# A decoder trunk on Trainium2: the low parts of its weights by an accumulating transfer in place of a subtraction on GpSimd

## The chip, the cores and the metric

The kernel runs on one core of a Trainium2 chip. The metric is the time of one execution in device microseconds (us). Lower is better. The engines are named as the profile names them: PE is TensorE (PEld its weight loads), DVE is VectorE, ACT is ScalarE, POOL is GpSimd, SP is SyncE (SPq its queue of transfers).

## What is computed

Four layers of a decoder over 1024 tokens of width 1024, in float32. The mixer of layer i is of kind i mod 3: gated linear attention (layers 0 and 3), a spatial gating unit (layer 1), forgetting attention (layer 2).

```
for i in range(DEPTH):                                   # DEPTH = 4
    mod = (silu(c) @ w_mod[i] + b_mod[i])[:, None, :]
    shift, scale, gate = split(mod, 3)
    h = rms_norm(x, norm_pre_g[i]) * (1.0 + scale) + shift
    kind, j = i % N_MIXERS, i // N_MIXERS
    ...                                                  # o = mixer(h @ w_in), times silu(z), @ w_out
    x = x + gate * rms_norm(o, norm_post_g[i])
```

The products `h @ w_in` and `o @ w_out` carry most of the work: w_in has 3088, 3072 or 4112 columns, w_out 1024.

## The kernel before

**Three matmuls for one.** The projections run in float32r, in which one matmul takes less time than in float32 but rounds its operands. Both operands are split into a rounded high part and a low part, the remainder: activations into hTh and hTl, weights into whi and wlo. `mm3` (L283) sums three products: high by high (L285), and the two of high by low (L286, L287). `proj_tok` (L289) and `proj_feat` (L324) call it for eight slices of the inner dimension (kt 0 to 7) and leave the sum in a PSUM bank (pool pj, three banks).

**Weights.** Each layer's weights are cut into blocks of about 256 columns, planned in order by `plan` (L273) and `plan_out` (L394). `getw` (L276) keeps one block ahead of the one in use. `load_w` (L246) fetches a block in two halves p4, each of 512 rows: a transfer by SyncE into a raw tile `wraw` (L263, 128 partitions x 4 x 256 floats, 512 KB), and then `split` (L251): ScalarE rounds the raw tile into the high part (L254), GpSimd subtracts it from the raw tile and writes the low part (L255). There are 176 halves in the program. The pool of `wraw` has two buffers, so a raw load waits until the subtraction two halves earlier has read its tile. The pool of `whi` and `wlo` (tag whl) has eight buffers, two for each half: a block in use and the next one. A cast therefore waits until the matmuls have done with the same half of the block two back. In the opening, wide transfers of the modulation weights (L182) use buffers of this pool too.

**Stages.** A layer runs through its input blocks, with the mixer's work put between the projections, and then through `out_proj` (L399): two halves of the tokens, four blocks each, so eight blocks a layer; in each block four tiles of 128 tokens, 24 matmuls for a tile. After each tile VectorE multiplies the bank by the gate (L410) and ScalarE squares it (L412), both to free the bank. Beside it `post` (L422) adds the residual of the tokens finished before and prepares the next layer's activations.

**Other work named below.** L197 accumulates the modulation on VectorE. L580 is a running sum, L602 to L612 the scaled operands of the gated attention's scores, L623 their matmuls, L625 copies them from PSUM under a mask. L673 to L683 update and read the attention's state (L678 on VectorE). L387 and L474 are low parts of activations on VectorE. L536 copies a few columns of a projection. L983 copies the halves of a tile between partitions by transfers within SBUF (L1019 and L1020 wait for them).

**What sets the order.** The kernel is written for a scheduler that simulates the program on a timeline and lays down the order of each engine's instructions; places marked high priority (L409) are preferred, and each engine then works strictly in its order and waits on semaphores. Transfers are all issued by SyncE, in the order of its queue.

Of the kernel before, what the change touches and what calls it, by code (L numbers as in the profile page):

```python
# [8 lines left out]
F32 = mybir.dt.float32  # L9
F32R = mybir.dt.float32r  # L10
U8 = mybir.dt.uint8
AF = mybir.ActivationFunctionType
ALU = mybir.AluOpType
# [15 lines left out]
class Trunk:  # L29
# [216 lines left out]
    def load_w(self, srcs, now=True):  # L246
        nc = self.nc
        ncol = sum(s.shape[1] for s in srcs)
        raws, parts = [], []

        def split(raw):  # L251
            hi = self.wp.tile([P, 4, ncol], F32R, tag="whl", name=self.nm("whi"))
            lo = self.wp.tile([P, 4, ncol], F32R, tag="whl", name=self.nm("wlo"))
            nc.scalar.copy(hi, raw)  # L254
            nc.gpsimd.tensor_tensor(lo, raw, hi.bitcast(F32), op=ALU.subtract)  # L255
            parts.append((hi, lo))

        for p4 in range(2):
            raw = self.wp.tile([P, 4, ncol], F32, tag="wraw", name=self.nm("wraw"), bufs=2)
            c = 0  # L260
            for s in srcs:
                w = s.shape[1]
                nc.sync.dma_start(out=raw[:, :, c:c + w],  # L263
                                  in_=s[p4 * 512:(p4 + 1) * 512, :].rearrange("(k p) n -> p k n", p=P))
                c += w
            if now:
                split(raw)
            else:
                raws.append(lambda raw=raw: split(raw))
        self.wdone.append(lambda kt: (parts[kt // 4][0][:, kt % 4, :], parts[kt // 4][1][:, kt % 4, :]))  # L270
        return raws
# [960 lines left out]
```

## Time and profile before

| | us |
|---|---|
| median of three runs | 2159.36 |
| lowest and highest | 2156.47 and 2163.68 |
| the profiled execution | 2157.83 |
| its span, first to last instruction | 2156.1 |
| PE busy in the span | 2093.7 (97%) |
| DVE busy | 1323.0 (61%) |
| ACT busy | 942.5 (44%) |
| POOL busy | 884.0 (41%) |
| mean busy share of the DMA engines, by SyncE's queue | 33.1% |

Busy time says how much of the span an engine held instructions. Matmuls overlap each other, so that PE counts as busy while it is only filled. What an engine that is not PE costs is read from the waits of PE, and those in turn from the timeline around them. The granted clock over the span is 0.992 of the full one.

### The profile page before, as it was taken

To read this page: it belongs to the slowest core of one execution; us is meant where nothing else is said; L and a number is where in the kernel's file an instruction comes from. 1 tells how busy PE (TensorE), PEld (TensorE's weight loads), DVE (VectorE), ACT (ScalarE), POOL (GpSimd) and SP (SyncE) were. 2 spreads that over 40 slices of the span, in tenths; PEclk is the share of its full clock that TensorE was granted. 3 is DMA by queue.
4 is the path that set the end of the run, shared out by engine and by line. 5 is a ranking of instruction groups with operands and counts; after the bars stand their busy time and mean duration, and the time that the engine had idled before them with its cause. 6 is when DMAs were issued, how large, how long until landed. Compare 5 with 4: busy or idle time off the path is not lost.

```text
span 2156.1 us, 39182 instructions
## 1 busy us (share of the span) xinstructions
PE 2093.7 (97%) x15173; PEld 1934.2 (90%) x15173; DVE 1323.0 (61%) x2940; ACT 942.5 (44%) x2041; POOL 884.0 (41%) x751
## 2 busy tenths in 40 slices
PE   6999999999999999999999999999899999999998
PEld 6888999999998889998888888888689999899998
DVE  7686878535475425555656656656766674776633
ACT  4655334345422114554445445445555655343342
POOL 5443333366344333645343244243326441332363
PEclk9999999999999999999999999999999999999999
DMA  8132323335425432524223224223425320111334
GB/s 291 40 93 74 94 85 98 122 115 180 146 77 160 143 105 98 175 83 109 74 74 109 79 69 115 72 70 108 134 88 196 100 59 21 50 59 55 118 106 144
DMA packets 183268, 225.91 MB, mean 105 GB/s; under 512 B 14290, under 2 KB 129554, under 8 KB 183082
## 3 DMA queue, kind: packets, MB, share of 16 engines
q1 hardware_dynamic: 183082, 223.41, 33.1%
q8 instruction: 119, 1.95, 0.4%
q14 instruction: 67, 0.55, 0.1%
HBM read 185.03 MB, written 29.95 MB: 100 GB/s over the span
## 4 chain that ended last, share of the span: by engine, by line
PE 83%; DVE 10%; ACT 2%; issue 2%; DMA 2%; POOL 0%; DVEq 0%; SPq 0%; POOLq 0%; ACTq 0%
PE pj L285 21%; PE pj L287 21%; PE pj L286 21%; PE pm L1056 4%; PE pm L1045 3%; PE pb L623 2%; DVE md L197 2%; PE pb L1019 2%; PE pb L1020 1%; DVE s L580 1%; DMA s<-s 1%; PE pm L364 1%; PE pm L683 1%; PE pm L682 1%; DVE s L612 1%
## 5 line engine op out<-in xcount | busy, mean ns | idle before, releaser
L285 PE MATMUL pj<-whi,hTh 128*128 128x256 f32 (+1 forms) x3072 | 891.8, 290 | 2.9 <-ACT junk L412 1.9
L287 PE MATMUL pj<-whi,hTl 128*128 128x256 f32 (+1 forms) x3072 | 880.7, 287 | 4.4 <-DVE hTl L474 2.1
L286 PE MATMUL pj<-wlo,hTh 128*128 128x256 f32 (+1 forms) x3072 | 881.2, 287 | 0.0
L255 POOL TENSOR_TENSOR wlo<-wraw,whi 128x1024 fp32r<-128x1024 f32 (+2 forms) x176 | 423.3, 2415 | 434.6 <-ACT whi L254 397.9
L285 PEld LDWEIGHTS pj<-whi,hTh 128*128 128x128 f32 x3072 | 590.3, 192 | 10.7 <-issue 3.3
L287 PEld LDWEIGHTS pj<-whi,hTl 128*128 128x128 f32 x3072 | 589.2, 192 | 10.0 <-DVE hTl L474 3.1
L286 PEld LDWEIGHTS pj<-wlo,hTh 128*128 128x128 f32 x3072 | 590.4, 192 | 5.3 <-issue 2.4
L285 PE MATMUL pj<-hTh,whi 128*128 128x512 f32 x640 | 255.3, 399 | 0.0
L287 PE MATMUL pj<-hTh,wlo 128*128 128x512 f32 x640 | 254.1, 397 | 0.0
L286 PE MATMUL pj<-hTl,whi 128*128 128x512 f32 x640 | 253.1, 395 | 0.0
L254 ACT CAST whi<-wraw 128x1024 fp32r<-128x1024 f32 (+2 forms) x176 | 178.0, 1012 | 110.2 <-PE pj L286 92.8
L197 DVE SCALAR_TENSOR_TENSOR md<-md,cond,md 128x512 f32<-128x512 f32 x184 | 171.2, 932 | 36.0 <-DMA md<-in_w_mod 34.1
L1013 POOL TENSOR_TENSOR db<-s,mneg 128x128 f32<-128x128 f32 x128 | 69.1, 548 | 271.0 <-DVE mx L1028 158.2
L1047 ACT COPY s<-pm 128x512 f32<-128x512 f32 (+2 forms) x192 | 87.6, 480 | 127.2 <-PE pm L1045 125.0
L287 PEld LDWEIGHTS pj<-hTh,wlo 128*128 128x128 f32 x640 | 120.8, 189 | 24.7 <-issue 0.9
L286 PEld LDWEIGHTS pj<-hTl,whi 128*128 128x128 f32 x640 | 121.0, 189 | 23.9 <-issue 0.7
L285 PEld LDWEIGHTS pj<-hTh,whi 128*128 128x128 f32 x640 | 120.9, 189 | 23.7 <-issue 0.7
L410 DVE TENSOR_TENSOR s<-pj,gg 128x256 f32<-128x256 f32 x128 | 53.5, 420 | 132.1 <-PE pj L287 132.0
L1034 ACT ACTIVATE p<-p,ng 128x256 f32<-128x256 f32 (+7 forms) x128 | 99.5, 777 | 79.5 <-DVE ng L1032 78.6
L1023 DVE CUSTOM_DVE_ANT_0 p<-pb,s 128x512 f32<-128x512 f32 (+3 forms) x160 | 82.4, 526 | 61.3 <-PE pb L1020 58.6
L1132 ACT ACTIVATE s<-pj 128x256 f32<-128x256 f32 (+1 forms) x96 | 43.8, 457 | 165.7 <-PE pj L287 157.6
L340 POOL TENSOR_TENSOR r<-r,neghalf 128x1 f32<-128x1 f32 (+2 forms) x104 | 113.0, 1092 | 6.7
(202 smaller groups left out, 3237.3 us busy)
## 6 DMA issues: line engine op xcount, KB each, us to landing
md<-in_w_mod SPq DMA_DIRECT2D x160, 256.0 KB
wraw<-in_gla_w_in SPq DMA_DIRECT2D x32, 512.0 KB
wraw<-in_gla_w_out SPq DMA_DIRECT2D x32, 512.0 KB
yd<-s SPq DMA_DIRECT2D x50, 256.0 KB
xd<-x SPq DMA_DIRECT2D x24, 512.0 KB
wraw<-in_sgu_w_in SPq DMA_DIRECT2D x24, 512.0 KB
x<-xd SPq DMA_DIRECT2D x24, 512.0 KB
wraw<-in_fox_w_in SPq DMA_DIRECT2D x48, 256.0 KB
```

Of the source, the lines that this page charges most:

```text
L197: ins = nc.vector.scalar_tensor_tensor(st["acc"], w[i], self.cond[:, kt:kt + 1], st["acc"], op0=ALU.mult, op1=ALU.add)
L254: nc.scalar.copy(hi, raw)
L255: nc.gpsimd.tensor_tensor(lo, raw, hi.bitcast(F32), op=ALU.subtract)
L285: nc.tensor.matmul(ps, lh, rh, start=first, stop=False)
L286: nc.tensor.matmul(ps, lh, rl, start=False, stop=False)
L287: nc.tensor.matmul(ps, ll, rh, start=False, stop=last)
L340: nc.gpsimd.tensor_tensor(r, r, self.half[:, 0:1].to_broadcast([P, n]) if n > 8 else self.half[:, 0:n], op=ALU.pow)
L1013: nc.gpsimd.tensor_tensor(db, nf[p, ib // 4, hb][:, qc], mneg, op=ALU.add)
L1023: nc.vector.tensor_tensor_reduce(e[:, c * 512:c * 512 + d0], sp[:, 0:d0], nf[p, c, hb][:, 0:d0], op0=ALU.add, op1=ALU.max, scale=1.0, scal ...
L1034: nc.scalar.activation(e[:, 0:n + P], e[:, 0:n + P], AF.Exp, bias=ng, accum_out=ls[:, 0:1])
L1047: nc.scalar.copy(et[:, 0:nb * P], pt[:, 0:nb * P])
L1056: nc.tensor.matmul(po[own[hb], 0:P], v[p, jb // 4][:, jb % 4, hb * 64:hb * 64 + 64], pts[hb][jb // 4][:, (jb % 4) * P:(jb % 4 + 1) * P], s ...
```

## The change

`split` computes the low part in another way. ScalarE writes, beside the rounded copy, the negated rounded copy of the raw tile into `wlo`. Then a transfer issued by GpSimd adds the raw tile onto `wlo` in SBUF, so that raw minus high part stands there. The transfer's completion, in place of the subtraction's end, now frees the raw tile and releases the matmuls of L286 (L287 in `proj_feat`). Behind L255 all line numbers grow by one.

```
             nc.scalar.copy(hi, raw)
-            nc.gpsimd.tensor_tensor(lo, raw, hi.bitcast(F32), op=ALU.subtract)
+            nc.scalar.activation(lo, raw, AF.Copy, scale=-1.0)
+            nc.gpsimd.dma_start(out=lo, in_=raw, accum_op=ALU.add)
             parts.append((hi, lo))
```

ScalarE in the second half of layer 0's output projection, before; whi and wraw are the parts and the raw tile of a weight half, junk and so the outputs of the squares:

```order
L412 ACTIVATE junk,so_692_4455<-pj_4705 128x256
L254 CAST whi_4761<-wraw_4759 128x1024
L254 CAST whi_4767<-wraw_4765 128x1024
L412 ACTIVATE junk,so_693_4456<-pj_4732 128x256
L412 ACTIVATE junk,so_690_4453<-pj_4771 128x256
```

and of the changed kernel:

```order
L413 ACTIVATE junk,so_692_4481<-pj_4735 128x256
L254 CAST whi_4791<-wraw_4789 128x1024
L255 ACTIVATE wlo_4792<-wraw_4789 128x1024
L254 CAST whi_4798<-wraw_4796 128x1024
L255 ACTIVATE wlo_4799<-wraw_4796 128x1024
L413 ACTIVATE junk,so_693_4482<-pj_4762 128x256
```

A negation now stands behind each cast, the first of them ahead of the second cast. GpSimd at the same place, before:

```order
L504 TENSOR_TENSOR hTl<-s_727_4701,hTh 128x4x128
L255 TENSOR_TENSOR wlo_4762<-wraw_4759,whi_4761 128x1024
L255 TENSOR_TENSOR wlo_4768<-wraw_4765,whi_4767 128x1024
L255 TENSOR_TENSOR wlo_4882<-wraw_4879,whi_4881 128x1024
L255 TENSOR_TENSOR wlo_4888<-wraw_4885,whi_4887 128x1024
```

and of the changed kernel:

```order
L505 TENSOR_TENSOR hTl<-s_727_4731,hTh 128x4x128
L256 DMA wlo_4792<-wraw_4789 128x1024
L256 DMA wlo_4799<-wraw_4796 128x1024
L256 DMA wlo_4914<-wraw_4911 128x1024
L256 DMA wlo_4921<-wraw_4918 128x1024
```

A DMA stands where each subtraction stood. SyncE's queue a little later in the same stage, before; x is the residual's tile, xd the layer's output in DRAM:

```order
L263 DMA wraw_5017<-in_gla_w_out 128x4x256
L442 DMA xd_130<-x_5050 128x1024
L428 DMA x_5069<-in_x 128x1024
L442 DMA xd_130<-x_5052 128x1024
L263 DMA wraw_5208<-in_gla_w_out 128x4x256
L263 DMA wraw_5214<-in_gla_w_out 128x4x256
L428 DMA x_5113<-in_x 128x1024
```

and of the changed kernel:

```order
L264 DMA wraw_5052<-in_gla_w_out 128x4x256
L443 DMA xd_130<-x_5086 128x1024
L429 DMA x_5105<-in_x 128x1024
L443 DMA xd_130<-x_5088 128x1024
L429 DMA x_5149<-in_x 128x1024
L264 DMA wraw_5244<-in_gla_w_out 128x4x256
L443 DMA xd_130<-x_5105 128x1024
```

The second load of x has moved ahead of the raw load that stood before it.

## Rows read from the trace of the kernel before

**Rows 1.** The page: engines' busy time, share and instructions; the chain by engine.

```profile
PE 2093.7 (97%) x15173; PEld 1934.2 (90%) x15173; DVE 1323.0 (61%) x2940; ACT 942.5 (44%) x2041; POOL 884.0 (41%) x751
...
PE 83%; DVE 10%; ACT 2%; issue 2%; DMA 2%; POOL 0%; DVEq 0%; SPq 0%; POOLq 0%; ACTq 0%
```

**Rows 2.** Groups by line: form, count | busy us, mean ns | idle before, what ended it.

```profile
L286 PE MATMUL pj<-wlo,hTh 128*128 128x256 f32 (+1 forms) x3072 | 881.2, 287 | 0.0
L255 POOL TENSOR_TENSOR wlo<-wraw,whi 128x1024 fp32r<-128x1024 f32 (+2 forms) x176 | 423.3, 2415 | 434.6 <-ACT whi L254 397.9 <-DMA s<-yd 18.3 <-PE pj L287 8.0
L254 ACT CAST whi<-wraw 128x1024 fp32r<-128x1024 f32 (+2 forms) x176 | 178.0, 1012 | 110.2 <-PE pj L286 92.8 <-issue 6.5 <-DVE SH L211 3.0
```

**Rows 3.** Waits of PE over the span: us in total, times, longest us.

```profile
PE pb L623 <- DVE cmix L625: 6.2, 5, 3.8
PE pm L682 <- DVE st L678: 4.2, 3, 2.4
...
PE pb L1019 <- DMA s<-s: 3.5, 6, 1.1
...
PE pb L623 <- DVE s L612: 2.8, 3, 2.4
PE pb L1019 <- DVE mx L1023: 2.7, 3, 1.5
PE pj L287 <- DVE hTl L474: 2.1, 2, 1.7
PE pj L287 <- DVE hTl L387: 2.1, 2, 1.5
...
PE pm L541 <- DVE al L536: 1.8, 1, 1.8
```

**Rows 4.** Timeline around 365 us, of POOL, DVE and PE: start, duration, instruction.

```profile
364.91 5.42 POOL L255 TENSOR_TENSOR wlo<-wraw,whi 128x1024 fp32r<-128x1024 f32 x2 [0.28 <-ACT whi L254]
...
365.50 2.60 DVE L608 TENSOR_TENSOR s<-s,qk 128x256 f32<-128x256 f32 x1
368.02 2.59 DVE L612 TENSOR_TENSOR s<-s,qk 128x256 f32<-128x256 f32 x1
...
371.72 0.70 PE L682 MATMUL pm<-st,s 128*128 128x256 f32 x2 [2.39 <-DVE st L678]
```

**Rows 5.** The opening: timeline of POOL; pieces of the chain (start, duration).

```profile
15.20 2.98 POOL L255 TENSOR_TENSOR wlo<-wraw,whi 128x1088 fp32r<-128x1088 f32 x1
...
16.15 2.59 DVE md L197
18.77 0.76 DVE md L197
...
30.64 2.86 DVE md L197
```

**Rows 6.** Stretches: us, busy by engine, granted clock, DMA share, GB/s.

```profile
479.50:491.10 11.60, 11.60 (x100) 11.60 (x99) 7.95 (x13) 5.12 (x15) 7.84 (x8) 1.00 0.61 200
...
447.85:448.90 1.05, 1.05 (x11) 1.05 (x11) 0.00 (x0) 0.00 (x0) 1.05 (x1) 1.00 0.00 0
448.90:451.20 2.30, 2.30 (x22) 2.30 (x20) 1.12 (x2) 1.10 (x3) 2.30 (x2) 1.00 0.76 228
```

**Rows 7.** Line L254 by itself: who waited for it (us, times).

```profile
  PEld pm L1056: 0.8, 5
```

**Rows 8.** Timeline of an output projection: ACT, POOL, SyncE's queue.

```profile
456.93 1.05 ACT L254 CAST whi<-wraw 128x1024 fp32r<-128x1024 f32 x1 [0.37 <-issue]
...
468.45 1.05 ACT L254 CAST whi<-wraw 128x1024 fp32r<-128x1024 f32 x1 [0.37 <-issue]
...
458.05 4.76 POOL L255 TENSOR_TENSOR wlo<-wraw,whi 128x1024 fp32r<-128x1024 f32 x2 [2.65 <-ACT whi L254]
...
460.49 2.72 SPq L263 DMA_DIRECT2D wraw<-in_gla_w_out  x2
```

**Rows 9.** Waits of SyncE's queue: us in total, times, longest us.

```profile
SPq L263 <- POOL wlo L255: 718.0, 118, 38.1
```

## The prediction

> **What bounds the kernel now.** I read the page first. TensorE is busy for 2093.7 of 2156.1 us, and the chain that ended last is 83% PE and 10% DVE [rows 1]. So the kernel ends when its stream of matmuls ends, and a change elsewhere shows only where the matmul stream stands still or is made to. The profiled execution took 2157.83 us (1.7 us outside its span); the median of the three timed runs is 2159.36 us, 0.07% above it.
>
> Second, the groups by line. The subtraction that goes, L255, takes 423.3 us of GpSimd in 176 instructions of 2415 ns, and its idle time mostly ends with the cast of the same weights on ScalarE (L254, 1012 ns). The matmuls that use its result (L286) never stand idle before them: 0.0 us [rows 2]. As work, then, the subtraction is hidden; shortening it alone would give nothing.
>
> Third, TensorE's waits over the whole span. Seven of them end with VectorE: 6.2 + 4.2 + 2.8 + 2.7 + 2.1 + 2.1 + 1.8 = 21.9 us. The longest that ends with a transfer within SBUF comes to 3.5 us [rows 3].
>
> Fourth, why VectorE is late there. Around 365 us two VectorE instructions on 256 columns take 2.60 and 2.59 us, one after the other, exactly while GpSimd runs two subtractions in a row (5.42 us from 364.91); the matmul behind them then waits 2.39 us [rows 4]. In the opening an L197 takes 2.59 us from 16.15 while a subtraction runs from 15.20 to 18.18, and the next L197 takes 0.76 us; another, at 30.64, takes 2.86 us [rows 5]. VectorE instructions that read two tiles in SBUF stand still until the subtraction is over. This is where the subtraction costs something.
>
> **The change part by part.** *Removed:* 176 subtractions, and with them those stalls of VectorE. Of the 21.9 us of waits I take three quarters, 16 us: the place in [rows 4] is of that kind, and so are the other waits for L678, L474, L387 and L536; some of those for L625 and L1023 are not, for no subtraction runs ahead of them. In the opening VectorE's L197 is on the chain, and two of them lose 2.59 - 0.76 = 1.8 and 2.86 - 0.76 = 2.1 us: 3.9 us. Together about 20 us, at most 26 (21.9 + 3.9) if every wait is of that kind, and less if the next instruction is late for another reason.
>
> *Added on ScalarE:* 176 instructions of the cast's size, 176 x 1.01 = 178 us. It lies beside the matmuls in stages where ScalarE is about half busy (5.12 of 11.60 us in a stretch of an output projection [rows 6]). What it costs is bounded by what the casts cost now: 0.8 us in 5 waits of TensorE's weight loads at the line that waits most for them [rows 7]. A pair twice as long might cost two or three times that; I put 2 us, between 0 and 5. In the opening each negation falls into gaps of ScalarE or moves work that VectorE holds up anyway: 0.
>
> *Added on the DMA engines:* 176 transfers, most of 512 KB (128 partitions x 1024 x 4 bytes). No row shows an accumulating transfer or one that GpSimd issues. Let X be the time from the end of the negation until the sum has landed. The nearest row is the load of one weight half: issued at 447.85, nothing moves for 1.05 us, then 512 KB in 2.3 us at 228 GB/s [rows 6], so 3.35 us. That is the low end. An accumulation reads two operands and writes one; if the two reads share what one load has, the data part doubles: 1.05 + 4.6 = 5.65 us. The high end is making the descriptors as slowly as the subtraction ran (2.4 us), 1.05 us of start and three passes of 2.3 us: 10.4 us. I take X = 5, nearer to the load, and keep 3.35 to 10.4 for the range.
> By the Trainium skill ("DMA: Bandwidth & Descriptors", Anatomy of one DMA, SWDGE path) a GpSimd-issued transfer takes 2.0 us plus its bytes at 436 GB/s, an estimate of 3.2 us here, and by "Collectives: The Full Stack" (The bandwidth ceiling) an add in the DMA engines is slower only because it reads two sources, which makes the estimate 4.4 us; no run here shows either yet, and the sum would be the same by it.
>
> *What X has to fit into.* The narrowest stage is the output projection: eight blocks a layer, four layers. A block lasts 11.52 us (one cast of its first half begins at 456.93, the next at 468.45 [rows 8]). There are two raw buffers, one for each half of a block. Before, the load into one is issued when its subtraction is over (460.49, when the first of the two L255 that begin at 458.05 has ended [rows 8]). After, the loop of one raw buffer is cast 1.05, negation 1.05, X, about 0.05 for the issue, load 3.35: 5.5 + X. It must fit into 11.52, so X may be 6.0. Up to there nothing moves. Beyond that each block of a layer comes later by X - 6.0. Against it stands a reserve. TensorE reaches a newly loaded half about 12.9 us after its cast begins, for the cast waits for the first half of the block two back, behind which stand half a tile (12 matmuls at 0.116 us, 1.4 us, from 100 in 11.60 us [rows 6]) and a whole block; less the cast and the negation, 10.8 - X is left. With the first two blocks of a layer loaded ahead, the loss is 4 x (6 x (X - 6.0) - (10.8 - X)): nothing up to X = 6.7, 9 us at 7, 37 at 8, 65 at 9, 93 at 10. At X = 5 it is zero, and the cover is thin: 1 us in the loop.
>
> *Behind the waiting instruction.* GpSimd's order keeps its place for place here, a DMA where the subtraction stood; behind it wait the small scale computations of the norms, which get free sooner if issuing is shorter than 2.4 us. SyncE now waits 718.0 us for subtractions ahead of its raw loads [rows 9]; after, it waits for the landing of the sum, later by 1.05 + X - 2.4 = 3.7 us each time, and what stands behind it goes later. In the output projection the scheduler has put one load of x ahead of a raw load, which helps x. In the forgetting attention the small transfers within SBUF stand in that queue and share the engines: the 3.5 us of waits may grow by half, 2 us.
>
> *In the opening* the new transfers meet DMA engines that are loading the modulation weights without a pause; one of them takes at least 2.3 us of their time, of which I let 1 us through to the end.
>
> Sum: 20 - 2 - 2 - 1 = 15 us off 2157.83 gives 2142.8, and 2144 from the median. I forecast **2143 us**.
>
> **The rivals.** *(a) The loop of the raw buffers becomes the bound, slower.* For it: X is only bounded, doubling the data part already brings 5.65 of the 6.0 that are free, and in blocks where x and the residual move too the DMA engines are at 0.61 and 200 GB/s already [rows 6]. Against it: up to 6.7 nothing is lost, and in all of these stretches the granted clock is 1.00, so the blocks don't get shorter [rows 6]. From X = 7.3 the loss (17 us) passes the gain. At X = 9 the loss is 65 us, and the time 2157.8 - 15 + 65 = 2208 us.
> The Trainium skill ("SBUF — State Buffer", the "DVE blocks DMA" trap) speaks for this rival: GpSimd can't write descriptors while VectorE runs an instruction that takes both of its ports; if one L197-sized instruction of 0.76 us stands ahead, X is 5.8, still inside the loop.
>
> *(b) VectorE gets nothing back.* Writing descriptors could hold VectorE off for as long as the subtraction did, or the stalled instructions could have had slack that the waits of the matmuls hide. Then the 20 us stay and the 5 us of costs are added or vanish in the noise: 2157.8 to 2163 us, no change. Against it: issuing moves no tile through GpSimd.
>
> *(c) The gain is larger.* Many waits under the resolution of the wait view go as well, as VectorE is delayed by every subtraction in the attention layers and not only by those that end in a listed wait. All 21.9 + 3.9 us and no costs: 2132 us, and a few more.
>
> *(d) The change does not do what it says* (the low part of the negated copy not equal to minus the high part, so a different number of instructions or a second transfer): the edit is one line for one line, and I see no sign of it; 2%, counted under (a).
>
> **How the numbers follow.** Forecast and (c) together 0.54 (X up to 6.7, the stalls gone), (b) with X up to 6.7: 0.14, (a) and (d): 0.32, of which 0.02 lies where loss and gain about cancel. A measurement of this kernel tells about 0.3% (6.5 us) from no change. So faster 0.54, same 0.16, slower 0.30. The range should leave out at most 2 in 10: downward to 2127, five below (c); upward into (a) to X of about 10, 2157.8 - 15 + 93 = 2236. The likeliest case's own range is 2127 to 2152.
>
> **What the profile after would show.** The stalls: L197, L608 and L612 without instructions of 2.5 us, VectorE's busy time down, and the waits of TensorE for L678, L536, L474 and L387 gone. The new instruction: about 1.05 us on ScalarE, 176 times. X: the time from a negation's end to the next raw load on SyncE in an output projection, 5 expected; if it is over 6.7, casts there wait for raw loads instead of for matmuls, and the blocks grow beyond 11.5 us. GpSimd's busy time should fall by about 423 us, with the issuing not counted. The prediction is wrong if the matmuls of the output projections wait for the low parts (rival a), if VectorE's long instructions stay (b), or if ScalarE's doubled work shows in the waits of the matmuls by more than 5 us.

## The result and the profile after

The changed kernel takes 2174.15 us (median of five runs, 2168.89 to 2176.42) against 2158.63 us: 1.0067 times as long, with a 95% interval of 1.0053 to 1.0081. It is **slower by 15.5 us**, where 15 us faster was forecast; the measured time lies inside the range, on the side of the other sign. The profiled execution took 2173.74 us, its span 2172.0 us.

The page of the changed kernel: engines, the chain by engine, the two DMA queues (packets, MB, share of 16 engines), and three groups (busy us, mean ns | idle before and what ended it). Lines behind L255 are one higher than in the rows of before.

```profile
PE 2094.7 (96%) x15173; PEld 1936.3 (89%) x15173; DVE 1184.9 (55%) x2940; ACT 1097.9 (51%) x2217; POOL 610.7 (28%) x751
...
q1 hardware_dynamic: 183082, 223.41, 32.5%
q0 software_dynamic: 25344, 88.29, 23.1%
...
PE 74%; DMA 12%; DVE 4%; ACT 4%; issue 4%; POOL 1%; SPq 0%; POOLq 0%; DVEq 0%; ACTq 0%
...
L287 PE MATMUL pj<-wlo,hTh 128*128 128x256 f32 (+1 forms) x3072 | 883.1, 288 | 4.4 <-DMA wlo<-wraw 4.3
...
L256 POOL DMA_DIRECT2D wlo<-wraw x176 | 156.2, 887 | 648.3 <-ACT wlo L255 563.6
...
L255 ACT ACTIVATE wlo<-wraw 128x1024 fp32r<-128x1024 f32 (+2 forms) x176 | 179.4, 1019 | 0.1
```

Against [rows 1], VectorE is busy 138 us less and ScalarE 155 us more, as the change asks for. GpSimd is busy 273 us less and not 423, because this page counts the issuing of the transfers (L256, 0.89 us each). The chain has gone from 2% DMA to 12%. And PE is busy as long as before, in a span that is 16 us longer: it stands still 77.3 us instead of 62.4.

Its waits over the whole span (us in total, times, longest us), to be read beside [rows 3]:

```profile
PE pj L286 <- ACT junk L413: 18.4, 11, 3.4
PE pb L1020 <- DMA s<-s: 6.7, 6, 2.9
...
PE pb L1021 <- DMA s<-s: 6.5, 4, 2.6
PE pj L287 <- DMA wlo<-wraw: 4.3, 3, 2.4
PE pb L624 <- DVE s L613: 4.3, 3, 2.5
```

The waits for the state (L678 before, L679 now) are gone and those for the low parts of activations are down to 0.4 us; the one for L613 (L612 before) is not gone, 4.3 us against 2.8. In place of the others stands one large new item, the wait for L413. That is ScalarE's square, the last reader of a PSUM bank of an output projection. It costs ScalarE 0.38 us, as before. It is late. Before, the same wait was small:

```profile
PE pj L285 <- ACT junk L412: 1.9, 2, 1.3
```

Why, at one of these waits: PE and ScalarE around 489 us in layer 0's output projection (start, duration, instruction, idle before and what ended it).

```profile
487.46 0.28 PE L288 MATMUL pj<-whi,hTl 128*128 128x256 f32 x1
489.61 0.38 PE L286 MATMUL pj<-whi,hTh 128*128 128x256 f32 x1 [1.86 <-ACT junk L413]
...
486.41 0.61 ACT L384 CAST hTh<-s 128x512 fp32r<-128x512 f32 x1
488.13 1.04 ACT L254 CAST whi<-wraw 128x1024 fp32r<-128x1024 f32 x1 [1.11 <-DMA wraw<-in_gla_w_out]
489.08 0.38 ACT L413 ACTIVATE junk<-pj 128x256 bf16<-128x256 f32 x1
```

ScalarE's next instruction is the cast of a weight half, whose raw tile hasn't landed. It waits 1.11 us, runs 1.04 us, and only then comes the square for which PE has been waiting since 487.7. No low part is late here: the raw load is, and it blocks ScalarE's queue.

Where the time went by stage, from the first to the last L410 (L411) of each layer's output projection; the last column adds the tail. The scheduler lays a new order for each kernel, so a few us of one stage may be chance.

| us | to layer 0's output proj. | the four output proj. with tail | SGU, layer 1 | FoX, layer 2 | GLA, layer 3 |
|---|---|---|---|---|---|
| before | 435.7 | 402.9 | 296.5 | 650.7 | 370.2 |
| after | 422.8 | 427.5 | 299.8 | 656.1 | 365.9 |
| e2, no transfer | 418.6 | 400.3 | 297.0 | 642.5 | 362.4 |
| e5, control of e6 | 422.2 | 429.7 | 299.5 | 669.2 | 364.4 |
| e6, three raw buffers | 422.3 | 403.8 | 299.3 | 667.7 | 361.5 |
| e11, VectorE | 420.3 | 398.2 | 299.2 | 644.5 | 361.5 |

The gain that was forecast is there, 12.9 us by the time layer 0's output projection begins and 4.3 us in layer 3. The four output projections lose 24.6 us, and the forgetting attention and the gating unit 8.7 us.

### The profile page after: what moved, and what is told of

It reads as the page before. It is cut to its first block, busy times and chain, and to the rows that moved or that the text cites. A ratio compares the mean times of both kernels' runs of the same rounds, so it can differ in the third digit from the quotient of the medians.

```text
span 2172.0 us, 39546 instructions
## 1 busy us (share of the span) xinstructions
PE 2094.7 (96%) x15173; PEld 1936.3 (89%) x15173; DVE 1184.9 (55%) x2940; ACT 1097.9 (51%) x2217; POOL 610.7 (28%) x751
## 3 DMA queue, kind: packets, MB, share of 16 engines
q0 software_dynamic: 25344, 88.29, 23.1%
## 4 chain that ended last, share of the span: by engine, by line
PE 74%; DMA 12%; DVE 4%; ACT 4%; issue 4%; POOL 1%; SPq 0%; POOLq 0%; DVEq 0%; ACTq 0%
PE pj L286 18%; PE pj L287 18%; PE pj L288 18%; DMA wlo<-wraw 5%; PE pm L1057 4%; PE pm L1046 3%; PE pb L624 2%; PE pb L1020 2%; PE pb L1021 1%; DMA md<-in_w_mod 1%; PE pm L684 1%; ACT wlo L255 1%; PE pm L674 1%; PE pm L683 1%; DMA s<-s 1%
## 5 line engine op out<-in xcount | busy, mean ns | idle before, releaser
L286 PE MATMUL pj<-whi,hTh 128*128 128x256 f32 (+1 forms) x3072 | 894.7, 291 | 19.8 <-ACT junk L413 18.4
L287 PE MATMUL pj<-wlo,hTh 128*128 128x256 f32 (+1 forms) x3072 | 883.1, 288 | 4.4 <-DMA wlo<-wraw 4.3
L286 PEld LDWEIGHTS pj<-whi,hTh 128*128 128x128 f32 x3072 | 592.5, 193 | 30.9 <-ACT junk L413 21.6
L287 PEld LDWEIGHTS pj<-wlo,hTh 128*128 128x128 f32 x3072 | 592.4, 193 | 9.7 <-DMA wlo<-wraw 5.2
L256 POOL DMA_DIRECT2D wlo<-wraw x176 | 156.2, 887 | 648.3 <-ACT wlo L255 563.6
L254 ACT CAST whi<-wraw 128x1024 fp32r<-128x1024 f32 (+2 forms) x176 | 177.5, 1009 | 155.7 <-PE pj L287 58.3
L286 PE MATMUL pj<-hTh,whi 128*128 128x512 f32 x640 | 255.2, 399 | 0.0
L287 PE MATMUL pj<-hTl,whi 128*128 128x512 f32 x640 | 252.0, 394 | 0.0
L197 DVE SCALAR_TENSOR_TENSOR md<-md,cond,md 128x512 f32<-128x512 f32 x184 | 143.1, 779 | 67.4 <-DMA md<-in_w_mod 65.5
L255 ACT ACTIVATE wlo<-wraw 128x1024 fp32r<-128x1024 f32 (+2 forms) x176 | 179.4, 1019 | 0.1
L1014 POOL TENSOR_TENSOR db<-s,mneg 128x128 f32<-128x128 f32 x128 | 64.6, 512 | 297.3 <-DVE mx L1029 185.6
L288 PEld LDWEIGHTS pj<-hTh,wlo 128*128 128x128 f32 x640 | 120.3, 188 | 24.6 <-issue 0.2
L286 PEld LDWEIGHTS pj<-hTh,whi 128*128 128x128 f32 x640 | 120.3, 188 | 24.2 <-issue 1.2
L287 PEld LDWEIGHTS pj<-hTl,whi 128*128 128x128 f32 x640 | 120.4, 188 | 23.8 <-issue 0.9
L411 DVE TENSOR_TENSOR s<-pj,gg 128x256 f32<-128x256 f32 x128 | 53.7, 421 | 148.2 <-PE pj L288 147.9
```

The source lines that it names most:

```text
L197: ins = nc.vector.scalar_tensor_tensor(st["acc"], w[i], self.cond[:, kt:kt + 1], st["acc"], op0=ALU.mult, op1=ALU.add)
L255: nc.scalar.activation(lo, raw, AF.Copy, scale=-1.0)
L256: nc.gpsimd.dma_start(out=lo, in_=raw, accum_op=ALU.add)
L286: nc.tensor.matmul(ps, lh, rh, start=first, stop=False)
L287: nc.tensor.matmul(ps, lh, rl, start=False, stop=False)
L288: nc.tensor.matmul(ps, ll, rh, start=False, stop=last)
```

## The experiments

Theories: **A**, the loop of a raw buffer is too long; **B**, ScalarE's added work delays the squares; **C**, the transfer's fixed cost; **D**, the DMA engines are full. All times are medians; the kernel before stood at 2158 to 2159 us beside each run.

**A copy in place of the addition.**

```
-            nc.gpsimd.dma_start(out=lo, in_=raw, accum_op=ALU.add)
+            nc.gpsimd.dma_start(out=lo, in_=raw)
```

> The changed kernel with one word less: the transfer onto the low part copies the raw tile instead of adding it, in the same order on every engine; so the low part holds the raw weights (the subtraction is left out). The changed kernel takes 2174 us; its waits of the matmuls for L413 (squares on ScalarE, which free the PSUM banks) are 18.4 us, against 1.9 us before, and its packets of the accumulating transfer take about 337 ns for 4 KB. Theory A, the loop: a raw buffer comes free late because the addition takes long (4.9 us from the end of the negation to the next load, and loads slowed by the other half's addition); the cast then waits for its load, and the squares behind it in ScalarE's order wait too. With a copy the packets should take about half, the loop gets 1 to 1.5 us shorter, and most of the 18 us go: 2150 to 2162 us. Theory B, ScalarE's own added work (176 negations, 179 us) is what delays the squares: nothing changes, 2170 to 2176 us. Theory C, the transfer's fixed cost (issue by GpSimd, start, completion) rather than the addition: 2165 to 2175 us, with the same loop.

2132.17 us, ratio 0.9878 (0.9858 to 0.9897): 42 us less than the changed kernel, with the same instructions in the same order. Its queue and its transfer by the page (KB each, median us from issue to landing), and then its wait for the squares:

```profile
q0 software_dynamic: 25344, 88.29, 12.3%
...
wlo<-wraw POOLq DMA_DIRECT2D x154, 512.0 KB, 3.5
```

```profile
PE pj L286 <- ACT junk L413: 3.8, 2, 2.0
```

The changed kernel's transfer takes 5.5 us to land, and its packets 23.1% of a longer span, 1.9 times as much. So it is the adding that loses the time, 2 us a transfer, and neither ScalarE (B) nor the fixed cost of a transfer from GpSimd (C). Theory A had expected 2150 to 2162 us; the copy gained more.

**No transfer at all.** The line with the transfer is taken out; ScalarE's negation stays.

> The changed kernel without the transfer onto the low part: the low part holds the negated rounded raw weights, the addition of the raw weights is left out; ScalarE's two instructions stay. It shows what all of the removed GpSimd work was worth and what ScalarE's added work costs, together. If the additions cost 30 us and the removed subtractions gave 20 us (so far the changed kernel is 14.6 us ahead of the kernel before when layer 0's output projection begins, and loses 6 to 10 us in each output projection), 2135 to 2142 us, with almost no wait for L412's squares. If ScalarE's negations are the cost (theory B), 2160 to 2172 us.

2121.30 us, ratio 0.9825 (0.9808 to 0.9842). Without GpSimd's subtraction, and with ScalarE's new work, the kernel is 37.8 us faster; the accumulating transfers give back 52.9 us. The kernel is 14 us faster than the lower end of what was expected. B falls here too: all negations are there, and one wait of 0.8 us is all that is left for a square. The engines by its page, and that wait:

```profile
PE 2081.5 (98%) x15173; PEld 1928.5 (91%) x15173; DVE 1177.7 (56%) x2940; ACT 1097.0 (52%) x2217; POOL 455.8 (21%) x575
...
PE pb L1019 <- ACT junk L412: 0.8, 1, 0.8
```

**ScalarE's negation alone,** added to the kernel before, ahead of the subtraction that overwrites it.

```
             nc.scalar.copy(hi, raw)
+            nc.scalar.activation(lo, raw, AF.Copy, scale=-1.0)
             nc.gpsimd.tensor_tensor(lo, raw, hi.bitcast(F32), op=ALU.subtract)
```

> The kernel before with the added negation on ScalarE and the subtraction on GpSimd still there, overwriting it: it prices ScalarE's added instruction alone. By the prediction 2 us (0 to 5): 2157 to 2165 us. If it is what the output projections lose (theory B), 2170 us or more. The run without a transfer, at 2121 us, has the same negations and almost no wait for a square, which already speaks against B.

2162.77 us, ratio 1.0017 (1.0004 to 1.0030): 1 to 6 us for 180 us of work.

**Half the change at a time.** In e4 the input projections use the accumulating transfer and the output projections the subtraction; e12 is the reverse. The line of e4 that chooses is shown; the flag's way through `plan` and `load_w` is left out.

```
-                self.plan([w_out[:, cb * 256:(cb + 1) * 256]])
+                self.plan([w_out[:, cb * 256:(cb + 1) * 256]], acc=False)
```

> Accumulating transfer for the input projections of all layers, subtraction on GpSimd as before for the output projections. If the loss lies in the output projections alone (6.7, 10.2, 7.7 and 6 us of the four of the changed kernel) and the gain in the gated attention's input stages (about 21 us), it is 2140 to 2147 us, faster than both. If the loss is spread (the forgetting attention's small transfers within SBUF wait 13.2 us in the changed kernel against 6.4 us before), 2148 to 2158 us.

> The other half of the change alone: the accumulating transfer for the output projections, the subtraction on GpSimd for all input projections. The accumulating transfer in the input projections alone gained 14.7 us (2144.4), the whole change lost 15.5 us (2174.2). If the loss sits in the output projections and the two parts add up, 15.5 + 14.7 = 30 us more than before: 2183 to 2193 us, with the waits for the squares back at 15 us or more. If the loss needs both parts (the additions of the stage after an output projection crowding the engines), clearly less: 2160 to 2180 us.

e4: 2144.41 us, ratio 0.9937 (0.9916 to 0.9957), faster than both kernels. e12: 2195.12 us, ratio 1.0170 (1.0148 to 1.0192), 37.5 us slower, with these waits (its line numbers are five higher than the changed kernel's here: L418 is the square, L292 reads the low part):

```profile
PE pj L291 <- ACT junk L418: 23.9, 16, 4.3
...
PE pj L292 <- DMA wlo<-wraw: 4.4, 3, 2.4
```

Most of the loss belongs to the output projections. The two parts add up to 23 us where the change as a whole loses 15.5; they are not quite independent, and why e12 loses more there than the whole change was not tried apart.

**A third raw buffer.** It fits only if the pool of small tiles shrinks from 28 to 25 buffers, so the control e5 has the smaller pool with two raw buffers.

```
-        self.sp = pool("sp", 28)
+        self.sp = pool("sp", 25)
...
-            raw = self.wp.tile([P, 4, ncol], F32, tag="wraw", name=self.nm("wraw"), bufs=2)
+            raw = self.wp.tile([P, 4, ncol], F32, tag="wraw", name=self.nm("wraw"), bufs=3)
```

> The changed kernel with 25 in place of 28 buffers in the pool of the small and middle tiles, which makes room for the third raw buffer of the next run; its control. All theories: 2170 to 2185 us; the smaller pool costs little or nothing.

> The control with three raw buffers in place of two, and nothing else. Theory A (a raw buffer's loop of cast, negation, addition and load is longer than half a block's turn): the loop may last half as long again, the loads go out earlier and the waits for the squares (18.4 us in the changed kernel) go: 15 to 30 us less than the control. Theory D (the DMA engines are full in the output projections: 2.7 us of all sixteen for one addition, against 1.4 us for one load): an earlier load competes with the additions just as now, and the sum stays: within 6 us of the control, with waits for low parts taking the place of those for the squares. The run that copies in place of adding gained 42 us, which fits both; the one that reads DRAM again lost 12.5 us, which speaks for D, though its packets are of 1 KB and take 102 ns each, 408 ns for 4 KB.

The control takes 2194.04 us: the smaller pool alone costs 20 us, where little or nothing was expected. Its profiled execution was its fastest and is 13 us longer than the changed kernel's; all of this lies in the forgetting attention. With the third raw buffer it is 2157.07 us, **37 us less**. Of the difference between the two profiled spans (30.5 us) the output projections have 25.9. In the control, the wait of PE for the squares, and what ScalarE's casts (line L254 by itself) waited for (us, times):

```profile
PE pj L286 <- ACT junk L413: 18.8, 15, 2.7
```

```profile
  PE pj L287: 52.1, 45
  DMA wraw<-in_gla_w_out: 30.3, 10
...
  DMA wraw<-in_sgu_w_out: 14.1, 8
```

The same two with the third raw buffer:

```profile
PE pj L286 <- ACT junk L413: 3.2, 2, 2.3
```

```profile
  PE pj L287: 64.9, 65
  DMA wraw<-in_gla_w_out: 8.7, 4
...
  DMA wraw<-in_sgu_w_out: 2.6, 2
```

The casts wait for PE again, as in the kernel before. The DMA engines were not the bound: they do more per us now. A stretch in the output projections of layers 0 and 1, in the control and with the third buffer, where the stretches reach 4 and 16 us past the end of these stages (us, busy by engine, granted clock, DMA share, GB/s):

```profile
422.00:523.00 101.00, 97.63 (x815) 96.98 (x814) 37.58 (x79) 59.54 (x131) 37.28 (x48) 1.00 0.81 205
824.00:924.00 100.00, 93.59 (x747) 92.34 (x746) 37.80 (x81) 60.60 (x132) 27.45 (x40) 0.97 0.86 220
```

```profile
422.00:523.00 101.00, 101.00 (x849) 100.91 (x848) 38.33 (x82) 62.62 (x136) 38.37 (x50) 1.00 0.88 223
824.00:924.00 100.00, 99.89 (x833) 99.59 (x832) 44.07 (x99) 67.28 (x144) 34.02 (x53) 1.00 0.95 251
```

At a share of 0.88 and 0.95 PE is busy throughout; at 0.81 and 0.86 it is not. Nor did the parts of the loop get shorter: over the 64 raw loads of output weights, the time from a negation's end to the next load is 6.3 us on average in the control and 6.3 with the third buffer, the load itself 4.9 and 5.0. Theory A holds, D falls as the first cause. One reservation: the third buffer also changes the order that the scheduler lays down for every engine but GpSimd, and the two were not separated. The copy, which has the changed kernel's order instruction by instruction, needs no such reservation.

**Raw tile freed early.** The addition reads DRAM again instead of the raw tile (the loop over a block's sources is left out here).

```
-            nc.gpsimd.dma_start(out=lo, in_=raw, accum_op=ALU.add)
...
+                nc.gpsimd.dma_start(out=lo[:, :, c:c + w], accum_op=ALU.add,
+                                    in_=s[p4 * 512:(p4 + 1) * 512, :].rearrange("(k p) n -> p k n", p=P))
```

> The changed kernel, but the accumulating transfer reads the weights from DRAM a second time instead of from the raw tile. The output is complete. The raw tile is then free when the negation on ScalarE has read it; the low part still comes from an accumulating transfer of the same size. Theory A (the raw buffer's loop is what is lost): the loop becomes cast, negation, load, about 7 of 11.5 us, the waits for the squares go below 5 us, 2140 to 2155 us. Theory D, the capacity of the DMA engines (additions and loads together fill them in the output projections): the same number of bytes and packets stays, waits move but do not go, 2165 to 2185 us, with waits of L287 for the low part in place of those for the squares.

2186.65 us, ratio 1.0123 (1.0093 to 1.0153). The squares are nearly on time (2.3 us of waits); now the low parts are late (L292 reads them in this kernel). The queue's share and two of its transfers by the page, and then two of the waits:

```profile
q0 software_dynamic: 112992, 88.29, 28.4%
...
wlo<-in_gla_w_in POOLq DMA_DIRECT2D x32, 512.0 KB, 8.3
wlo<-in_gla_w_out POOLq DMA_DIRECT2D x32, 512.0 KB, 9.2
```

```profile
PE pj L292 <- DMA wlo<-in_gla_w_out: 6.5, 5, 2.0
PE pj L292 <- DMA wlo<-in_sgu_w_in: 6.4, 2, 3.4
```

The loop is shorter, but an addition of 1 KB packets from DRAM takes 8 to 9 us to land. It was read as a sign for D; after e6 it only says that this form of the transfer is slower still. How much of that is the packets and how much the crowd was not separated.

**Four raw buffers of half the size.** Load, cast, negation and addition each run on half a tile.

> The changed kernel with its raw weights in four buffers of half the size in place of two: the same memory, the same bytes, twice as many loads, casts, negations and additions, each of half the size. Theory A (the loop of a raw buffer): a buffer is used once in a block of 11.5 us instead of once in one too, but its loop holds only half a load and half an addition, about 0.6 + 0.6 + 3.5 + 2.5 = 7.2 us: the waits for the squares go, as with the third buffer, which gained 37 us over its control: 2135 to 2150 us. Theory D (capacity of the DMA engines): 2172 to 2190 us. Against it in either: 352 instructions of fixed cost more on ScalarE, and twice as many of GpSimd's issues (0.88 us each).

2194.25 us, ratio 1.0158 (1.0129 to 1.0186): the expectation was wrong. Half the bytes take 4.7 us to land instead of 5.5, ScalarE has 33 us and GpSimd 156 us more to do, and the wait for the squares is 19.2 us, where the changed kernel has 18.4. The scheduler also casts the two halves in a row, so that each buffer waits for its twin. It shortened the loop hardly, and so tells little on A.

**Better versions.** e10 keeps the transfer for the gated attention's input projections alone, e7 is e4 with the output projections' subtraction on VectorE, e11 is the kernel before with all subtractions on VectorE:

```
-            nc.gpsimd.tensor_tensor(lo, raw, hi.bitcast(F32), op=ALU.subtract)
+            nc.vector.tensor_tensor(lo, raw, hi.bitcast(F32), op=ALU.subtract)
```

> The accumulating transfer for the input projections of the two layers of gated attention alone, the subtraction on GpSimd everywhere else. From the stages of the run with it in all input projections (2144 us): 15.1 and 5.4 us are gained in front of the output projections of layers 0 and 3, 6.7 us lost in the spatial gating unit, 0.3 us lost in the forgetting attention. If these stages are independent, 2135 to 2141 us; if the 6.7 us were a chance of the scheduler's order, 2141 to 2148 us.

> As the run with the accumulating transfer for the input projections alone (2144 us), but the output projections' subtraction on VectorE in place of GpSimd: 64 instructions of some 1.2 us, estimated from the subtraction of 128 x 512 on VectorE in the changed kernel (about half of that). VectorE is busy about 45 of 100 us there. If what those stages still lose in that run is VectorE standing still beside GpSimd, 2136 to 2142 us; if the order of VectorE (the subtraction ahead of the instructions that free the PSUM banks) costs as much as GpSimd's neighbourhood did, 2144 to 2150 us.

> The kernel before with the subtraction on VectorE in place of GpSimd, with no negation and no transfer: the third way to be rid of the subtraction on GpSimd. 176 instructions of about 1.2 us add some 200 us to VectorE, which gets back about 140 us that it lost beside GpSimd (busy 1323 us before, 1185 us in the changed kernel). If what the change gains (38 us when the transfer costs nothing) is VectorE's freedom, this keeps part of it: 2130 to 2150 us. If the subtractions hold up the short instructions of the chains on VectorE: 2150 to 2170 us.

e10: 2135.22 us, 0.9894 (0.9875 to 0.9913). e7: 2145.85 us, 0.9946 (0.9927 to 0.9965), no better than e4. **e11: 2123.41 us, 0.9834 (0.9817 to 0.9850)**, better than expected and the fastest kernel that computes everything, 2 us above the one that leaves the additions out. Its page, first the engines and then VectorE's new group:

```profile
PE 2081.2 (98%) x15173; PEld 1927.6 (91%) x15173; DVE 1373.9 (65%) x3116; ACT 946.4 (45%) x2041; POOL 478.1 (23%) x575
...
L255 DVE TENSOR_TENSOR wlo<-wraw,whi 128x1024 fp32r<-128x1024 f32 (+2 forms) x176 | 210.9, 1201 | 100.5 <-ACT whi L254 98.3
```

VectorE does in 1.20 us what took GpSimd 2.42 us, and no longer stands still beside it: 211 us of work cost it 51 us of busy time more than before.

## Why the prediction was wrong, point by point

**The stalls of VectorE: right, and under-priced.** In the kernel before, 27 instructions of L197 that overlap a subtraction last 1.78 us on average and 119 that overlap nothing on GpSimd 0.75 us; in the changed kernel 26 that overlap an L256 last 0.75 us as well. So rival (b) falls. The Trainium skill ("SBUF — State Buffer", Who interferes with whom) has an instruction with two SBUF inputs on VectorE contend with a GpSimd instruction that reads SBUF, which these numbers show; its "DVE blocks DMA" trap shows no delay in the issuing here, since L256 takes 0.83 to 1.10 us all through; whether a landing was delayed by it was not tried apart.

The forecast gave 20 us for this and at most 26. e2 gained 37.8 us, ScalarE's 1 to 6 us already paid, and so more than rival (c) allowed. PE's standing still went from 62.4 to 39.1 us, 23.3 us less, and 19.9 us of it had ended with VectorE: the waits had been read rightly. What made the price too low is that a wait was priced at its own length. PE's busy time fell by another 12.2 us, and the granted clock rose from 0.992 to 0.995 of full, which is (0.008 x 2156) - (0.005 x 2121) = 6.6 us. Behind some waits of PE, not all, the granted clock is at half. Two stretches of the kernel before, the first just behind the wait of 2.38 us for L612 that ends at 206.3, the second behind one of 1.5 us for L991 (us, busy by engine, granted clock, DMA share, GB/s):

```profile
206.60:210.00 3.40, 3.40 (x11) 2.81 (x11) 3.40 (x10) 1.73 (x3) 0.46 (x1) 0.50 0.47 148
1537.80:1548.00 10.20, 9.12 (x46) 7.24 (x47) 7.67 (x25) 4.89 (x12) 3.04 (x4) 0.50 0.49 136
```

The other 5.6 us of busy time have no place in the trace that I could name.

**ScalarE: right.** 2 us were forecast, between 0 and 5; e8 has 1 to 6.

**X, the time of the addition: too low.** The timeline of the changed kernel in layer 0's output projection, of ScalarE, GpSimd and SyncE's queue:

```profile
455.85 1.05 ACT L254 CAST whi<-wraw 128x1024 fp32r<-128x1024 f32 x1 [0.62 <-DMA wraw<-in_gla_w_out]
456.80 1.05 ACT L255 ACTIVATE wlo<-wraw 128x1024 fp32r<-128x1024 f32 x1
...
467.66 1.05 ACT L254 CAST whi<-wraw 128x1024 fp32r<-128x1024 f32 x1 [0.79 <-DMA wraw<-in_gla_w_out]
468.61 1.05 ACT L255 ACTIVATE wlo<-wraw 128x1024 fp32r<-128x1024 f32 x1
...
483.81 1.05 ACT L254 CAST whi<-wraw 128x1024 fp32r<-128x1024 f32 x1 [3.27 <-DMA wraw<-in_gla_w_out]
...
458.14 0.86 POOL L256 DMA_DIRECT2D wlo<-wraw  x1 [8.93 <-ACT wlo L255]
...
462.70 3.90 SPq L264 DMA_DIRECT2D wraw<-in_gla_w_out  x2
...
477.77 0.38 SPq L264 DMA_DIRECT2D wraw<-in_gla_w_out  x1
```

The first negation ends at 457.85, the next load into that tile is issued at 462.70: X = 4.85, and 5.0 had been taken. But this is the shortest X of the stage. One turn later the negation of that tile ends at 469.66 and the load is issued at 477.77: X = 8.11. Over all 64 raw loads of output weights X lies between 4.6 and 10.2 us, 6.3 on average. It is longer where the residual's tiles move too: the chain holds a transfer of the other tile of 7.43 us and the load behind it of 5.65 us.

```profile
474.89 7.43 DMA wlo<-wraw
482.38 5.65 DMA wraw<-in_gla_w_out
```

By the Trainium skill ("DMA: Bandwidth & Descriptors", Anatomy of one DMA) the estimate was 3.2 us for a GpSimd-issued transfer; e1's copy lands in 3.5 us, which agrees. With the data part doubled for an add it was 4.4 us, and the median here is 5.5: 1.9 times the packet time fits the two reads, and the rest, which varies with what else moves, comes on top.

**The loop: both terms too small, and this turned the sign.** This is the step that failed: a loop of 5.5 + X with X = 5, so 10.5 us, that was to fit into the block's 11.52 us. The two turns of that tile take 467.66 - 455.85 = 11.81 us and 483.81 - 467.66 = 16.15 us, and before the third cast ScalarE stands idle for 3.27 us. On average over the 64 loads the loop is 2.0 for cast and negation, 6.3 for X and 5.0 for the load in place of 3.35, together 13.3 us. The load's price came from [rows 6], from a stretch in which nothing else moved. In the kernel before the same 64 loads already took 4.2 us on average, so half of what was missing there could have been read beforehand; the other half came with the additions that run beside them. With 5.0 us for the load the formula leaves X = 4.4, not 6.0, and the forecast's X of 5 was already beyond it. The cover of "1 us in the loop" was called thin and then counted as whole.

**The reserve: named at the wrong place.** The loss was to begin when low parts came late, with 10.8 - X us in hand. Only 4.3 us of waits are for low parts. What comes late first is ScalarE's cast, ahead of the squares in ScalarE's order, and behind the squares stand only three PSUM banks. So the loss begins with a late load. Rival (a) had the right loop, but its price from X = 6.7 on stood on this reserve. It cost 27 us in the output projections against e2. With the measured loop of 13.3 us and X of 6.3 the prediction's formula gives 4 x (6 x 1.8 - (10.8 - 6.3)) = 25 us; that the size agrees is in part luck, since the reserve in it is not what ran out.

**The smaller costs.** The transfers within SBUF of the forgetting attention: 2 us were added to the waits in the forecast; it was 13.2 - 6.4 = 6.8 us (L1020 and L1021, before L1019 and L1020). That stage is 13.6 us longer than in e2; what the other half of this is was not tried apart. The opening did not lose: layer 0's first projections begin at 46.9 us, before at 48.1.

## What to carry to other kernels

A transfer that replaces an instruction joins a loop of buffers: price each leg of that loop, the loads too, with the new transfer running beside it, and treat a margin smaller than this as none. Then ask which queue a late leg blocks: here it was not the consumer of the data, but an unrelated short instruction behind a waiting cast. And before work is taken off a slow engine by way of the DMA engines, try it on the engine that it was disturbing: VectorE did the subtraction at half the time and ended the disturbance as well.

## What was not expected of the hardware

The packets of an accumulating transfer within SBUF take 1.9 times as long on the DMA engines as those of a copy of the same bytes (23.1% of 2172 us against 12.3% of 2129 us for 176 of them), and it lands after 5.5 us instead of 3.5. With the third raw buffer the DMA engines stood at a busy share of 0.95 (251 GB/s) for 100 us, in which PE was idle for 0.1 us. And PE's granted clock was at half behind some short waits: this one of 1.78 us, in the changed kernel's layer 1, ends at 874.00, and the clock is 0.50 (1.2 of 2.4 GHz) in the second of the two stretches below (us, busy by engine, granted clock, DMA share, GB/s). A packet is counted where it starts, so the share of a short stretch can pass 1. Behind the wait of 1.86 us that ends at 489.61, shown above, it stayed at 1.00.

```profile
874.00 0.38 PE L286 MATMUL pj<-whi,hTh 128*128 128x256 f32 x1 [1.78 <-ACT junk L413]
```

```profile
874.00:875.00 1.00, 1.00 (x8) 1.00 (x9) 1.00 (x2) 0.47 (x2) 0.78 (x1) 1.00 0.76 152
875.10:878.50 3.40, 3.40 (x19) 3.40 (x18) 0.55 (x2) 0.47 (x2) 0.00 (x0) 0.50 1.06 160
```
